# A two-layer hybrid decoder: one ordered set of weight tiles, another queue for blocks split ahead, and other part sizes in the middle of the FFN

## The chip, the cores and the metric

The kernel runs on one core of one Trainium2 chip. The metric is the device time of one execution in microseconds (us). Before the change it is 1271.52 us, the median of three runs (1269.11 to 1273.94).

## The reference, cut to what matters

Two layers, each a mixer sub-layer (attention, a Conformer convolution and a short gated convolution side by side) and a ConvGLU feed-forward network (FFN). 528 tokens (16 meta tokens and 512), width 1024, FFN width 2816, all in float32. The change lies in the FFN:

```python
D_MODEL, SEQ, N_META, DEPTH, D_FF, FFN_KERNEL = 1024, 512, 16, 2, 2816, 3

def ffn_sublayer(h, pre_g, post_g, w_up, conv_w, w_down):
    u = rms_norm(h, pre_g)
    z = jnp.einsum("bld,df->blf", u, w_up)            # (528, 5632)
    z = causal_depthwise_conv(z, conv_w)              # 3 taps
    g, up = jnp.split(z, 2, axis=-1)
    y = jnp.einsum("blf,fd->bld", jax.nn.silu(g) * up, w_down)
    return h + rms_norm(y, post_g)
...
    for l in range(DEPTH):
        h = mixer_sublayer(h, ...)
        h = ffn_sublayer(h, ...)
    return h[:, N_META:]
```

## The kernel before, in words

**Precision by halves.** Every float32 operand of a large product is split in two float32r tiles, a high part (a cast on ScalarE, ACT) and a low part (raw minus high, on VectorE, DVE). A product is three matmuls: high × high, low × high, high × low (`mm3`, L692). Weights arrive as blocks of 128 partitions × up to 1056 columns ("raw"), by DMA from one long array `wflat`, and are split on the way. Token columns lie in two halves of about 264.

**The order of the work** is made by a planner, `Flow` (L325 onwards): each operation of ACT, DVE, GpSimd and the DMA queues is given a planned cost, what it comes after, a priority and the ring slot that it takes, and is written out in the order in which the planner would run it. TensorE's work comes from generators ("threads"). The program order on each engine and queue is thus fixed in advance; on the chip, semaphores make each instruction wait for what it reads, and engines and queues run in order. `Ring` hands out buffers in turn, `Pick` (L202) the one that the plan has free first.

**The middle of the FFN** (`middle`, L2359) goes through the 22 pairs of gate and up blocks, in the order of `ORDERS`, in four parts of `PARTS` pairs:

- `u` is one plain up block: 48 matmuls, eight k × three products × two halves. Two of them make a pair (96 matmuls). The first two pairs are made before the middle starts (as `first`); the third (`h`) is made half by half as the normalised input u appears.
- `a` and `b` make a pair by a Strassen-Winograd scheme with seven products in place of eight: 7 × 12 = 84 matmuls (`eighth`, L2306). It needs weights X (one raw block), the sums Y and Z of quarter blocks (four DVE additions, L2199, into tile `z`), and W (half a raw block), each split in high and low, and four sums T of the input, made once a layer (`plan_t`, L2326, tiles `h` and `t_lo`). Between its products there are copies on ACT (L2454, L2460, L2469) and additions in PSUM on DVE (L2459, L2470, L2474).
- `D` is one of the eight blocks of the down projection for the part before: as many k as that part has pairs, added to `yp` by DVE (L2442).
- After each pair comes `gating` (L2249): two times (one tap on ACT, L2261, two on DVE, L2264) into one of four `c` tiles, SiLU (L2275), product (L2282, L2284), and the split into one of eight `g` tiles (yhi L2294, ylo L2298). A part's `g` tiles are given back with its eighth `D`.

The last part's down projection is made in `finish` (L1756), whose `products` follow the middle; post-norm, residual and the next layer's pre-norm are in it.

**Weights in the middle** are brought by `bring` (L2112; raw loads at L2120 on SyncE's queue, SPq, in three buffers `raw`) and split by `halves` (L2125; high L2132, low L2142) in five pairs of tiles (`general`), with a small ring for W (`wring`, the `acc` tiles) and one tile `z` for all four sums. `LOOK` is how many items ahead this is planned.

**Blocks split ahead.** In layer 1's middle, `split_ahead` (L2155) also splits the 22 blocks of layer 2's input projection, in 44 pieces: load `araw` (L2165), cast `ahi` (L2169), subtraction in place (L2173), and two stores to DRAM, `split_w` (L2175, L2177), all three DMAs on SPq. Two `araw` buffers and one `ahi` buffer turn over. Layer 2's mixer then fetches ready halves through GpSimd's queue (L636), which also carries other weights outside the middle (`plan_block`, L623). Two pieces are planned with each `D`.

**Between mixer and FFN**, `scaled_half` (L2040) makes u when the norm's factor rz is there: for each half 8 multiplications h × gain × rz on DVE (L2053), casts (L2056), subtractions (L2058). The residual h goes to DRAM (`h_mid`) and comes back for `finish`.

## Time and profile before

| | us |
|---|---|
| median of three runs | 1271.52 |
| the profiled execution, its own time | 1268.06 |
| its span, first to last instruction | 1266.3 |
| TensorE (PE) busy | 1230.4 |
| VectorE (DVE) busy | 1008.4 |
| ScalarE (ACT) busy | 709.3 |
| GpSimd (POOL) busy | 113.2 |

The mean granted clock of TensorE was 0.997 of full speed. Busy time of TensorE counts overlapping matmuls once, so a stretch that is all busy is told apart from a slow one by the number of matmuls in it. Layer 1's FFN starts at about 266 us and its Strassen pairs run from 322.67 to 578.28; layer 2's FFN starts at about 900 us. Rows of the profile name the line of the kernel, the engine, the operation and "written<-read" tiles; a queue's name ends in q (SPq, POOLq), and its rows are the issuing of DMAs.

### The profile page before, as it was taken

What the parts mean: (1) busy time and instruction counts of PE and PEld (TensorE: products, weight loads), DVE (VectorE), ACT (ScalarE), POOL (GpSimd) and SP (SyncE); (2) the same over time, 40 slices, a digit from 0 to 9 for tenths busy, and PEclk for the clock granted to TensorE, in tenths of its full rate; (3) what the DMA queues carried; (4) which work ended last, traced back from release to release, by engine and by line L of the source; (5) the groups of instructions that cost most, each with busy time, mean ns of one, the idle gap of its engine ahead of it and who ended that gap; (6) DMA issues with size and microseconds to landing.
All of it is one profiled execution on the core that took longest, in us unless ns stands there. A gap on an engine that the chain in (4) does not pass through costs nothing.

```text
span 1266.3 us, 24330 instructions
## 1 busy us (share of the span) xinstructions
PE 1230.4 (97%) x9552; PEld 1175.1 (93%) x9552; DVE 1008.4 (80%) x1785; ACT 709.3 (56%) x1389; POOL 113.2 (9%) x270
## 2 busy tenths in 40 slices
PE   9999999999999999989999999999999999999997
PEld 8988899989999999979999998999898998999897
DVE  7999986899978888876479985767998768887755
ACT  7446577666555555453563355776655444444543
POOL 1312210100000000000213133101000000000000
PEclk9999999999999999989999999999999999999999
DMA  7132123522476776665461652245222332323511
GB/s 253 51 86 77 52 76 119 184 85 88 154 250 231 227 234 219 220 236 191 163 254 34 195 154 78 88 145 184 69 80 84 125 101 75 106 90 99 189 58 67
DMA packets 75346, 173.22 MB, mean 137 GB/s; under 512 B 7984, under 2 KB 26672, under 8 KB 75232
## 3 DMA queue, kind: packets, MB, share of 16 engines
q1 hardware_dynamic: 61008, 119.01, 28.9%
q0 software_dynamic: 14080, 52.53, 12.8%
q8 instruction: 75, 1.23, 0.4%
q14 instruction: 39, 0.32, 0.1%
q10 hardware_dynamic: 144, 0.13, 0.1%
HBM read 135.49 MB, written 31.79 MB: 132 GB/s over the span
## 4 chain that ended last, share of the span: by engine, by line
PE 69%; DVE 18%; DMA 5%; ACT 4%; issue 3%; SPq 0%; DVEq 0%; ACTq 0%
PE psum L698 43%; PE psum L2310 14%; DVE c L2264 4%; PE psum L1325 3%; PE psum L1571 2%; DVE wlo L2142 2%; PE psum L1518 2%; DMA split_w<-ahi 2%; DVE z L2199 2%; DVE cacc L1044 2%; DMA raw<-in_w_dram 1%; DMA split_w<-araw 1%; PE psum L861 1%; PE psum L1473 1%; ACT whi L2132 1%
## 5 line engine op out<-in xcount | busy, mean ns | idle before, releaser
L698 PE MATMUL psum<-uhi,whi 128*128 128x264 f32 (+1 forms) x1120 | 288.4, 290 | 0.0
L698 PE MATMUL psum<-ulo,whi 128*128 128x264 f32 (+1 forms) x1120 | 281.5, 284 | 3.5 <-DVE ulo L2058 2.9
L698 PE MATMUL psum<-uhi,wlo 128*128 128x264 f32 (+1 forms) x1120 | 281.2, 284 | 0.0
L698 PE MATMUL psum<-yhi,whi 128*128 128x264 f32 (+3 forms) x928 | 260.3, 303 | 5.1 <-DVE c L2264 4.4
L698 PE MATMUL psum<-ylo,whi 128*128 128x264 f32 (+3 forms) x928 | 257.0, 300 | 1.5 <-DVE ylo L2298 1.1
L698 PE MATMUL psum<-yhi,wlo 128*128 128x264 f32 (+3 forms) x928 | 256.9, 299 | 0.6 <-DVE wlo L652 0.6
L698 PEld LDWEIGHTS psum<-ulo,whi 128*128 128x128 f32 x1120 | 196.0, 188 | 5.5 <-DVE ulo L2058 4.0
L698 PEld LDWEIGHTS psum<-uhi,whi 128*128 128x128 f32 x1120 | 196.3, 188 | 3.1 <-ACT uhi L2056 0.4
L698 PEld LDWEIGHTS psum<-uhi,wlo 128*128 128x128 f32 x1120 | 196.1, 188 | 0.0
L698 PEld LDWEIGHTS psum<-yhi,whi 128*128 128x128 f32 x928 | 166.5, 189 | 11.4 <-ACT rs L2460 4.8
L698 PEld LDWEIGHTS psum<-ylo,whi 128*128 128x128 f32 x928 | 166.5, 189 | 8.2 <-DVE ylo L2298 2.5
L698 PEld LDWEIGHTS psum<-yhi,wlo 128*128 128x128 f32 x928 | 166.5, 189 | 6.7 <-DVE wlo L652 1.2
L2264 DVE SCALAR_TENSOR_TENSOR c<-psum,pv,c 128x512 f32<-128x512 f32 (+2 forms) x160 | 117.8, 753 | 46.9 <-ACT c L2261 46.2
L636 POOL DMA_DIRECT2D raw<-in_w_dram x60 | 32.1, 536 | 911.9 <-DMA h<-h_mid 672.2
L2142 DVE TENSOR_TENSOR wlo<-raw,whi 128x1024 fp32r<-128x1024 f32 (+2 forms) x102 | 105.5, 1041 | 6.0 <-ACT whi L2132 5.8
L2132 ACT CAST whi<-raw 128x1024 fp32r<-128x1024 f32 (+2 forms) x102 | 92.0, 905 | 25.3 <-PE psum L698 17.2
L1044 DVE SCALAR_TENSOR_TENSOR cacc<-apad,pv,cacc 128x528 f32<-128x528 f32 x120 | 90.3, 766 | 1.2
L2261 ACT ACTIVATE c<-psum,pv 128x528 f32<-128x528 f32 (+1 forms) x80 | 55.0, 693 | 64.2 <-PE psum L2310 34.1
L652 DVE TENSOR_TENSOR wlo<-raw,whi 128x1024 fp32r<-128x1024 f32 (+3 forms) x66 | 74.6, 1142 | 17.8 <-ACT whi L646 17.5
L2310 PE MATMUL psum<-h,whi 128*128 128x264 f32 (+1 forms) x288 | 82.7, 287 | 5.8 <-ACT whi L2132 5.6
L2310 PE MATMUL psum<-h,wlo 128*128 128x264 f32 (+1 forms) x288 | 83.2, 289 | 5.2 <-DVE wlo L2142 5.1
L2310 PE MATMUL psum<-uhi,whi 128*128 128x264 f32 (+1 forms) x288 | 81.9, 284 | 0.9 <-DVE psum L2470 0.9
(263 smaller groups left out, 2589.1 us busy)
## 6 DMA issues: line engine op xcount, KB each, us to landing
raw<-in_w_dram SPq DMA_DIRECT2D x78, 512.0 KB, 3.6
raw<-in_w_dram POOLq DMA_DIRECT2D x44, 512.0 KB, 4.2
araw<-in_w_dram SPq DMA_DIRECT2D x40, 256.0 KB, 3.6
split_w<-ahi SPq DMA_DIRECT2D x40, 256.0 KB, 3.4
split_w<-araw SPq DMA_DIRECT2D x40, 256.0 KB, 4.3
raw<-in_w_dram SPq DMA_DIRECT2D x32, 320.0 KB, 2.9
whi<-split_w POOLq DMA_DIRECT2D x20, 512.0 KB, 4.7
wlo<-split_w POOLq DMA_DIRECT2D x20, 512.0 KB, 6.4
```

Source lines behind the costliest of these rows:

```text
L636: nc.gpsimd.dma_start(to, src)
L652: nc.vector.tensor_sub(box["lo"][:, a:z], box["raw"][:, a:z], box["hi"][:, a:z].bitcast(F32))
L698: nc.tensor.matmul(d, lhsT=w[a][:, k, cols], rhs=rhs(b, k, hf), start=start and i == 0 and p == 0, stop=stop and i == n - 1 and p == 2)
L1044: nc.vector.scalar_tensor_tensor(conv[j], in0=src, in1=conv[j], scalar=col("a_dw_w", CK * j + i), op0=ALU.mult, op1=ALU.add)
L1325: nc.tensor.matmul(ps[:n, :nw], lhsT=(uhi, ulo)[ui][:, k, P * b:P * b + n], rhs=w[wi][:, k % 4, :], start=k == 0 and p == 0, stop=k == KD ...
L1518: nc.tensor.matmul(s, lhsT=k[:, ka:ka + kn], rhs=q[:, s0:s1], start=i == 0, stop=i == 1)
L1571: nc.tensor.matmul(d[DH * e:DH * (e + 1)], lhsT=lhsT(hd), rhs=rhs(hd), start=start, stop=stop)
L2132: nc.scalar.copy(box["hi"], src())
L2142: b.tok = dve(dve_us(n), lambda: nc.vector.tensor_sub(box["lo"], src(), box["hi"].bitcast(F32)), c, prio=at(due_us + 1.0))
L2261: nc.scalar.activation(box["c"], src, AF.Copy, scale=wtap(2, t))
L2264: nc.vector.scalar_tensor_tensor(d, in0=src, scalar=wtap(i, t), in1=d, op0=ALU.mult, op1=ALU.add)
L2310: nc.tensor.matmul(dst, lhsT=w[a][:, k0 + k], rhs=rhs(b, k), start=start and k + p == 0, stop=stop and k == 3 and p == 2, skip_group_check ...
```

## The change

Part sizes go from 6, 5, 5, 6 to 5, 5, 5, 7. The number of Strassen pairs goes from 12 to 13 in layer 1 and from 12 to 15 in layer 2. A new letter `w` in the order says where two pieces are split ahead, in place of two with each `D`. The pieces' three DMAs go from SPq to GpSimd's queue. The weight tiles of the middle (raw, high, low and the half-size W) come from one set of 14 (15 in layer 2), and are taken in one order that is written down ahead from the planned begin of each item (`plan_order`): a take waits, in the plan, until the one before it in that order has been made. A load is planned `LOAD` before its item, sums `SUM` and high parts `HIGH` before it; a DMA's planned latency grows by `SLACK`. `LOOK` goes from 7 to 9. The one tile for the four sums becomes two (Z and Y apart). `scaled_half` multiplies by rz alone, two blocks at a time, on values already multiplied by the gain on ACT (`gained`, in `finish`). One weight block fewer is prepared before the middle. The last part's reload of h is planned after the last item of the middle instead of after the last Strassen pair.

```diff
-PARTS = (6, 5, 5, 6)
-ORDERS = [("uuuuuu", "aDbDaDbDaDbDuuaDbD", "aDbDaDbDaDbDuuaDbD", "aDbDaDbDaDbDaDbDuuuu"),
-          ("uuuuuu", "aDbDaDbDaDbDuuaDbD", "aDbDaDbDaDbDuuaDbD", "aDbDaDbDaDbDaDbDuuuu")]
-LOOK = 7
+PARTS = (5, 5, 5, 7)
+ORDERS = [("uuuu", "aDwbDwaDwbDwwaDwbDwwuwuwaDwbDwww", "aDwbDwaDwbDwaDwbDwuwuwaDwbDww", "aDbDaDbDaDbDaDbDaubuuu"),
+          ("uuuu", "aDbDaDbDaDbaDbaDbD", "aDbDaDbDaDbaDbaDbD", "aDbDaDbDaDbaDbaDbDuuuu")]
+LOOK = 9
+SLACK, LOAD, SUM, HIGH = 1.5, 16.0, 9.0, 7.0
...
     after_first = [next(i for i, c in enumerate(chunks) if ...) + FIRST["w_out"]
-                   + 3
+                   + 2
...
             def scaled_half(hf, r_at):
-                    fs = [dve(stt_us(n), lambda y=y, k=k, i=i: nc.vector.scalar_tensor_tensor(
-                        y[:, i, :], in0=h[:, k + i, a:z], scalar=g_u[:, k + i:k + i + 1], in1=rz[:, a:z],
-                        op0=ALU.mult, op1=ALU.mult), r_at, prio=1) for i in range(2)]
+                    fs = [dve(dve_us(2 * n), lambda y=y: nc.vector.tensor_mul(
+                        y, y, rz[:, a:z].unsqueeze(1).to_broadcast([P, 2, n])), r_at, *hg_at[hf, k], prio=1)]
...
             else:                                  # in finish, ends(hf)
+                for k in range(0, KD, 2):
+                    begun[hf, k] = gained(h, yp, a, z, k, gpre, out_at[hf, k], 0.9)
                 yield from norms.factor(("h", hf), n[hf], out=rz[:, a:z])
...
+            def place(buf, dt):
+                if buf < 9:
+                    return T(wp, [P, CHUNK], dt, f"{('raw', 'whi', 'wlo')[buf // 3]}{buf % 3}", 1)
+                if buf < 13:
+                    return T(wx[0], [P, WCHUNK], dt, f"{('whi', 'wlo')[(buf - 9) // 2]}{3 + (buf - 9) % 2}", 1)
+                if buf < 14:
+                    return T(fp, [P, 4 * H], dt, "acc", 1)
+                return T(t_pool[0], [P, WCHUNK], dt, f"more{buf}", 1)
+            def plan_order():
+                for j, (x, f, e) in enumerate(plan_list):
+                    w = begins[j]
+                    if x == "a":
+                        events.extend([(w - LOAD, j, "r0"), (w - LOAD, j, "r1"), (w - SUM, j, "xh"), (w - SUM, j, "xl"),
+                                       (w - HIGH, j, "zh"), (w - HIGH, j, "zl")])
+                    elif x == "b":
+                        events.extend([(w - HIGH, j, "yh"), (w - HIGH, j, "yl"), (w - HIGH + 2.0, j, "wt")])
+                    elif x == "d" or x == "u" and (f, e) not in early_up:
+                        events.extend([(w - LOAD, j, "r0"), (w - HIGH, j, "xh"), (w - HIGH, j, "xl")])
+                events.sort(key=lambda v: v[0])
+                for a, b in zip(events, events[1:]):
+                    turn[b[1:]] = a[1:]
+            def takes(j, key, slot):
+                before = turn[j, key]
+                wait = When(lambda: [] if before is None or before in taken else None)
+                return [wait], [(tiles[0], slot)]
+            def plain_block(j, i, when):
+                b = Block()
+                raw, s1, got, n = load(j, "r0", i, when - LOAD)
+                hi, s2, c = high(j, "xh", raw, n, when - HIGH, got)
+                until(b, s2, low(b, j, "xl", raw, hi, n, when - HIGH + 1.0, c))
+                s1.close(b.tok)
+                return b
...
             def split_ahead(due_us):
-                got = flow.op("sp", dma_us(z - a), load, prio=at(due_us), lat=dma_lat(z - a), takes=[(araws, slot)])
+                def queued(us, to, src, *after, **kw):
+                    def issue():
+                        flow.free["pool"] = max(flow.free.get("pool", 0.0), flow.now) + GP_DMA
+                        nc.gpsimd.dma_start(to(), src())
+                    return flow.op("wdma", dma_us(z - a), issue, after, prio=at(us), lat=dma_lat(z - a) + SLACK, **kw)
+                got = queued(due_us, raw, lambda: wflat[...][:, a:z], takes=[(araws, slot)])
...
-                hslot.close(flow.op("sp", ..., lambda: nc.sync.dma_start(home[i][0][:, a:z], box["hi"].bitcast(F32)), [d], ...))
-                slot.close(flow.op("sp", ..., lambda: nc.sync.dma_start(home[i][1][:, a:z], box["raw"]), [d], ...))
+                hslot.close(d, queued(due_us + 6.0, lambda: home[i][0][:, a:z], lambda: box["hi"].bitcast(F32), c))
+                slot.close(queued(due_us + 6.0, lambda: home[i][1][:, a:z], lambda: box["raw"], d))
...
                 elif x == "d":
-                    blocks[j] = plain_block(chunk_at["ffn_w_down", e, starts[f]], when)
-                    if l == 0:
-                        split_ahead(when)
-                        split_ahead(when + 2.0)
+                    blocks[j] = plain_block(j, chunk_at["ffn_w_down", e, starts[f]], when)
+                elif x == "w":
+                    split_ahead(when)
+                    split_ahead(when + 2.0)
...
             def middle():
-                        if j == last_b:
-                            wider[0].close()
-                            wx[1] = wider[0].enter_context(...)
-                            h_again.extend(load_h(fp, h_mid, 1.0))
-                            freed.append(p4)
+                        freed[:] = [p4]
                     yield
+                yield [*araws.slots, *ahis.slots]
+                wider[0].close()
+                wx[1] = wider[0].enter_context(...)
+                h_again.extend(load_h(fp, h_mid, 1.0))
```

More of the change, by code (lines that the diff above doesn't have):

```diff
@@ L809, in square @@
             if k == 0:
[L810 removed]
+                a = act(us, lambda: squares(lambda: self.acc_tile[:, slot.buf][:, :, :n]), *after,
                         prio=prio, takes=[(self.acc, slot)])
@@ L2147, in plain_block, with bring @@
-            def plain_block(i, due_us):
-                box, slot, got = bring(i, due_us - 12.0)
-                b = halves(lambda: box["raw"], chunks[i][3] * chunk_cols(chunks[i]), due_us - 6.0, got)
-                slot.close(b.tok)
+                def bring():
+                    box["t"] = took(j, key, slot, F32)[:, :sz]
+                    nc.sync.dma_start(box["t"], wflat[offs[i]:offs[i] + P * sz].rearrange("(p s) -> p s", p=P))
+                wait, take = takes(j, key, slot)
+                got = flow.op("sp", dma_us(sz), bring, wait, prio=at(due_us), lat=dma_lat(sz) + SLACK, takes=take)
@@ new lines, in load, with blocked, high, copy @@
+                return box, slot, got, sz
+            def blocked(t):
+                return t.rearrange("p (k n) -> p k n", n=P)
+            def high(j, key, src, n, due_us, *after):
+                box, slot = {}, Slot()
+                def copy():
+                    box["t"] = took(j, key, slot)[:, :n]
+                    nc.scalar.copy(box["t"], src["t"])
+                wait, take = takes(j, key, slot)
+                return box, slot, act(act_us(n), copy, *after, *wait, prio=at(due_us), takes=take)
@@ new lines, in low, with rest, until @@
+            def low(b, j, key, src, hi, n, due_us, *after):
+                slot = Slot()
+                wait, take = takes(j, key, slot)
+                def rest():
+                    lo = took(j, key, slot)[:, :n]
+                    nc.vector.tensor_sub(lo, src["t"], hi["t"].bitcast(F32))
+                    b.w = blocked(hi["t"]), blocked(lo)
+                b.tok = dve(dve_us(n), rest, *after, *wait, prio=at(due_us), takes=take)
+                return slot
+            def until(b, *slots):
+                for s in slots:
+                    s.close(b.slot)
@@ L2161, in split_ahead @@
                 box, slot, hslot = {}, Slot(), Slot()
-                def load():
-                    box["raw"] = T(t_pool[0], [P, CHUNK // 2], F32, "araw", 2)[:, :z - a]
-                    nc.sync.dma_start(box["raw"], wflat[offs[i]:offs[i] + P * sz].rearrange("(p s) -> p s", p=P)[:, a:z])
                 def high():
@@ L2192, in plan_item @@
                 elif x == "a":
-                    (b1, s1, got1), (b2, s2, got2) = (bring(chunk_at["ffn_w_up", f + NF * e, 0], when - 14.0) for e in range(2))
-                    box, zslot = {}, Slot()
-                    def summed(o, left, right, new=False):
-                        if new:
-                            box["s"] = T(fp, [P, 4, 2 + L], F32, "z", 1).rearrange("p a b -> p (a b)")
-                        nc.vector.tensor_add(box["s"][:, Q * o:Q * (o + 1)], left(), right())
-                    half = {name: (lambda b=b, o=o: b["raw"][:, Q * o:Q * (o + 1)])
-                            for name, b, o in (("11", b1, 0), ("12", b1, 1), ("21", b2, 0), ("22", b2, 1))}
@@ L2203, in plan_item @@
-                    sums = [lambda i=i: box["s"][:, Q * i:Q * (i + 1)] for i in range(4)]
-                    X = halves(lambda: b1["raw"], WCHUNK, when - 8.0, got1)
-                    sa = dve(dve_us(Q), lambda: summed(0, half["21"], half["22"], True), got2, prio=at(when - 8.0),
-                             takes=[(zring[0], zslot)])
-                    sc = dve(dve_us(Q), lambda: summed(1, half["21"], half["11"]), got1, sa, prio=at(when - 8.0))
-                    sb = dve(dve_us(Q), lambda: summed(2, sums[1], half["22"]), sc, prio=at(when - 7.9))
@@ L2209, in plan_item @@
-                    sd = dve(dve_us(Q), lambda: summed(3, sums[2], half["12"]), sb, prio=at(when - 7.9))
-                    Z = halves(lambda: box["s"][:, 2 * Q:4 * Q], WCHUNK, when - 6.0, sb, sd)
-                    s1.close(X.tok, sc, sd)
-                    quarters[f] = {"X": X, "Z": Z, "sums": (box, zslot, sa, sc, Z), "raw": (b2, s2)}
-                elif x == "b":
-                    q = quarters[f]
-                    box, zslot, sa, sc, Z = q["sums"]
-                    b2, s2 = q["raw"]
-                    q["Y"] = halves(lambda: box["s"][:, :2 * Q], WCHUNK, when - 6.0, sa, sc)
-                    zslot.close(q["Y"].tok, Z.tok)
-                    def small():
-                        return [T(fp, [P, 2, H], F32R, "acc", 2).rearrange("p a b -> p (a b)") for _ in range(2)]
-                    q["W"] = halves(lambda: b2["raw"][:, Q:], Q, when - 5.0, sa, ring=wring[0], tiles=small)
-                    s2.close(sa, sc, q["W"].tok)
+                    (r1, s1, got1, n), (r2, s2, got2, _) = (
+                        load(j, f"r{e}", chunk_at["ffn_w_up", f + NF * e, 0], when - LOAD) for e in range(2))
@@ L2503, in tile_hybrid_trunk @@
                        lambda k: y_at[k, 0] + y_at[k, 1], yp,
-                       gains("mix_post_g"), gains("ffn_pre_g"), SPLIT["w_out"], first, rz, scaled_half, early, middle())
+                       gains("mix_post_g"), gains("ffn_pre_g"), SPLIT["w_out"], first, rz, scaled_half, early, middle(), hg_at)
                 flow.yields = 2
-                flow.run(lambda: len(freed) and not flow.threads)
+                flow.run(lambda: len(h_again) and not flow.threads)
                 was = {s.buf: s for s in mids[0].slots}
```

161 lines of the change are left out of this document (97 added, 64 removed).

## The prediction

> **What bounds the kernel now.** I read the page's engine shares and chain first, then the busy time of each engine by stretch, then who waited for whom on TensorE and on SyncE's queue (SPq, which only issues DMAs), then the order of time at the places found.
>
> ```profile
> PE 1230.4 (97%) x9552; PEld 1175.1 (93%) x9552; DVE 1008.4 (80%) x1785; ACT 709.3 (56%) x1389; POOL 113.2 (9%) x270
> PE 69%; DVE 18%; DMA 5%; ACT 4%; issue 3%; SPq 0%; DVEq 0%; ACTq 0%
> 266.00:332.00 66.00, 63.51 (x505) 61.97 (x504) 64.50 (x98) 39.08 (x57) 0.00 (x0) 1.00 0.27 85
> 322.00:460.00 138.00, 133.34 (x1078) 131.66 (x1078) 113.49 (x164) 79.18 (x126) 0.00 (x0) 1.00 0.68 223
> 460.00:505.00 45.00, 45.00 (x371) 45.00 (x370) 37.68 (x55) 24.61 (x40) 0.00 (x0) 1.00 0.69 233
> 505.00:580.00 75.00, 66.73 (x517) 65.38 (x516) 58.59 (x87) 36.52 (x58) 0.00 (x0) 0.95 0.68 228
> 899.00:965.00 66.00, 63.26 (x495) 61.05 (x496) 63.99 (x99) 37.86 (x56) 0.00 (x0) 1.00 0.22 68
> 965.00:1043.00 78.00, 78.00 (x535) 72.52 (x535) 55.50 (x76) 38.99 (x59) 0.00 (x0) 1.00 0.36 113
> ```
>
> Columns: stretch, length, busy time (instructions) of PE, PEld, DVE, ACT, POOL, granted clock, DMA share, GB/s. TensorE is the bound: 371 matmuls in 45.00 us is 0.1213 us each with no gap. At that pace the 517 of 505–580 need 62.7 us, so 12.3 us are lost there, part of it as a lower clock (0.95); the 1078 of 322–460 need 130.8, so 7.2 are lost. Both lie in layer 1's FFN middle. Layer 2's (965–1043) has nearly no gaps. The two openings of the FFN (266–332, 899–965) differ: DVE is busy 64.50 and 63.99 of 66 us, so there DVE and TensorE are bounds side by side.
>
> Why 505–580 loses time:
>
> ```profile
> PE psum L2310 <- ACT whi L2132: 5.6, 2, 4.2
> ACT ahi L2169 <- DMA araw<-in_w_dram: 5.8, 2, 3.8
> ACT ahi L2169 <- DMA split_w<-ahi: 3.4, 2, 2.9
> SPq L2165 <- DMA split_w<-araw: 104.7, 40, 5.1
> SPq L2120 <- DVE z L2199: 13.6, 6, 11.0
> ```
>
> (Total us, times, longest.) TensorE waits for ScalarE's weight casts (whi). ScalarE takes its work in order and stands before `ahi`, the cast of a block split ahead for layer 2. That block's load and stores go out on SPq, which stood 104.7 us in all until a buffer's store had landed, before its next split-ahead load. The FFN's own weight loads (L2120) queue behind it.
>
> **The change, part by part.**
>
> *More Strassen pairs.* A plain up pair is 96 matmuls, a Strassen pair 84. The number goes from 12 to 13 in layer 1 and to 15 in layer 2: four pairs, 48 matmuls fewer.
>
> ```profile
> 578.28 35.07 PE psum L698 x288
> L2142 DVE TENSOR_TENSOR wlo<-z,whi 128x1024 fp32r<-128x1024 f32 x48 | 58.6, 1220 | 11.4 <-ACT whi L2132 11.3
> L2199 DVE TENSOR_TENSOR z<-z,raw 128x512 f32<-128x512 f32 x48 | 32.9, 686 | 0.6
> L2459 DVE TENSOR_TENSOR psum<-rs,psum 128x258 f32<-128x258 f32 x5 | 2.1, 429 | 0.1
> ```
>
> 35.07/288 = 0.1218 us each: **−5.8 us**, all on the path. The price lies on DVE: one more low part of 1.22, a small one and four sums of 0.69, three PSUM adds of about 0.43: some 6 us more per pair. In layer 2 a part like 965–1043 would go from 55.5 of 78 us to 61.5 of 76.5, or 80%. That is below the 84% (37.68 of 45.00) at which layer 1 ran without a gap in 460–505, so I cost it at nothing; without that cover it is 6 us × 4 pairs.
>
> *Blocks split ahead on GpSimd's queue.* 132 DMAs leave SPq, so the FFN's loads no longer wait behind a store, and GpSimd, with no work there (POOL 0.00 in the rows above), waits instead; behind it stand only other blocks and, after the middle, the last part's weight loads. The two `araw` buffers and the one `ahi` buffer stay, so ScalarE can still stand before `ahi`. The planner gives each transfer 1.5 us more (SLACK) and so puts the cast later. Bounds for 505–580: all 12.3 us come back, or a third (4), when ScalarE's 9.2 us of waits for `ahi` stay. The nearest row is 322–460, where the same work and the same queue cost 7.2 us, of which 2.2 and 0.8 have other causes (below): 4.2 in 138 us, or 2.3 in 75. I take **−10**; of the 4.2 themselves, which SPq causes only in part, **−1** (0 to −3).
>
> *Parts of 5 instead of 6 pairs first.*
>
> ```profile
> 1031.30 7.22 PE psum L2310 x60
> 1038.52 4.17 PE psum L698 x18
> 1039.25 1.31 ACT L2294 CAST yhi<-c 128x512 fp32r<-128x512 f32 x2
> 1044.50 1.27 ACT L2261 ACTIVATE c<-psum,pv 128x512 f32<-128x512 f32 x2
> PE psum L698 <- DVE c L2264: 4.4, 2, 2.2
> ```
>
> Part 1's last Strassen pair leaves TensorE at 1038.52, but its gating starts at 1044.50, and the next down block, which reads it, waits 2.2 us; the 4.4 are this place in both layers. The gating needs two of four `c` buffers; two earlier pairs hold them until they get a `g` tile, and there are eight `g` tiles, six held by part 0 up to its last down block (1038.52, then `yhi` at 1039.25). With five held, three are free for part 1, pair 4 holds two `c` and pair 5 has the other two. **−4.4**; between 0 (another holder is late next) and −5.2 with the two `ylo` waits behind it.
>
> *The opening of the FFN.* Part 0 loses a plain pair, which moves to the last part: 96 × 0.1218 = 11.7 us of TensorE work leave a stretch where DVE is full. What leaves DVE with it:
>
> ```profile
> L2142 DVE TENSOR_TENSOR wlo<-raw,whi 128x1024 fp32r<-128x1024 f32 (+1 forms) x9 | 10.4, 1159 | 0.0
> L2264 DVE SCALAR_TENSOR_TENSOR c<-psum,pv,c 128x527 f32<-128x527 f32 (+1 forms) x16 | 11.9, 760 | 0.0
> L2284 DVE TENSOR_TENSOR c<-c,c 128x528 f32<-128x528 f32 x6 | 4.2, 704 | 0.0
> L2298 DVE TENSOR_TENSOR ylo<-c,yhi 128x528 fp32r<-128x528 f32 x6 | 4.2, 703 | 0.0
> L2053 DVE SCALAR_TENSOR_TENSOR yp<-h,pg,rz 128x264 f32<-128x264 f32 x16 | 6.7, 488 | 0.0
> L2058 DVE TENSOR_TENSOR ulo<-yp,uhi 128x528 fp32r<-128x528 f32 x8 | 5.3, 705 | 0.6 <-ACT uhi L2056 0.6
> PE psum L2310 <- DVE wlo L2142: 0.8, 1, 0.8
> L1782 ACT ACTIVATE yp<-psum,pg 128x264 f32<-128x264 f32 (+1 forms) x32 | 13.8, 484 | 0.6 <-PE psum L698 0.6
> ```
>
> Busy time by count: 2 × 1.16 + 4 × 0.74 + 0.70 + 0.70 = 6.7 us. `scaled_half` replaces 16 multiplies (6.7) by 8 of the size of L2058 (5.3): 1.4. In layer 1 one split-ahead subtraction (0.7) goes to a later place. So DVE is done 8.8 us sooner in layer 1 and 8.1 in layer 2, TensorE 11.7, and the first Strassen pair waits already (0.8). TensorE stands 2.9 + 3.6 us more: **+6.5**. Bounds: 0, if DVE's order puts the first pair's weights ahead of all gating, and +10, if four taps (3.0) come before them. The gains that leave the multiply go to ScalarE, 16 of 0.484 a layer, at a priority ahead of the second half's squares; ScalarE is busy 39 of 66 us there. **+1**, 0 to +4.
>
> *Costed at nothing.* The weight tiles: 13 or so in rings become 14 (15) in one set; a Strassen pair with two down blocks takes 9 + 6 = 15 of them, about the old fill. The later reload of h (after the last item instead of the last Strassen pair): the next 210 matmuls, 25.6 us, run without it. The last part's seventh pair: 48 matmuls change places.
>
> Sum: −5.8 − 10 − 1 − 4.4 + 6.5 + 1 = **−13.7 us**. The profiled execution took 1268.06 us, which would become 1254.4; the median of the runs is 1271.52, 3.5 above it, and becomes **1257.8**.
>
> **The rivals.** (1) *The opening costs nothing*: DVE's order favours the pair. −20.2, 1251.3. For it: sums and low parts have due times of their own; against: DVE has no gap there.
>
> (2) *The end of layer 1's middle stays as it is.* The same bytes go through the same DMA engines, `araw` still has two buffers, and ScalarE still stands before `ahi` in order: term −10 becomes 0. −3.7, 1267.8, no change. For it: 9.2 us of waits for `ahi` in that stretch; against: SPq's 104.7 us. [...]
>
> (3) *The written tile order makes each pair wait.* One late load now holds up every take behind it, hi and low parts included. Place: the first matmuls of each of 28 Strassen pairs.
>
> ```profile
> PE psum L2310 <- DVE wlo L2142: 5.1, 7, 1.4
> ```
>
> At 5.1/7 = 0.73 us a pair this is 20.4 us: 1278.2, slower. It undoes the gain from 0.49 us a pair. Against: 15 takes on 14 tiles leave almost a whole stage of lead.
>
> (4) *GpSimd's queue is too slow for the blocks.*
>
> ```profile
> raw<-in_w_dram SPq DMA_DIRECT2D x78, 512.0 KB, 3.6
> raw<-in_w_dram POOLq DMA_DIRECT2D x44, 512.0 KB, 4.2
> split_w<-araw SPq DMA_DIRECT2D x40, 256.0 KB, 4.3
> wlo<-split_w POOLq DMA_DIRECT2D x20, 512.0 KB, 6.4
> L2173 DVE TENSOR_TENSOR araw<-araw,ahi 128x512 f32<-128x512 f32 x40 | 27.4, 686 | 16.8 <-ACT ahi L2169 16.8
> L2169 ACT CAST ahi<-araw 128x512 fp32r<-128x512 f32 x40 | 24.8, 620 | 26.1 <-DMA split_w<-ahi 19.4 <-DMA araw<-in_w_dram 6.7
> ```
>
> A buffer's turn is load + cast + subtract + store. At 4.2 and 4.3 it is 9.8 us, 4.9 a block with two buffers, 216 us for 44 blocks; at 6.4 for the store 6.0 and 262 us. Some 275 us are there: from about 311 (the first Strassen pair, 11.7 us sooner than now) to about 585 (the middle's last up block, now at 578.28 + 222 × 0.1218 = 605, less the 20 that leave it). At 7 us both ways it would be 337, 62 beyond; 25.6 of that is hidden, 36 show: 1294. It decides from 6.25 us a block. [...]
>
> **How the numbers follow.** About 0.5% (6.4 us) is what a measurement can tell from no change, so faster is below 1265.2. Chances: forecast 0.50 (own range 1252 to 1264), rival 1 0.18, rival 2 0.18, rival 3 0.09, rival 4 0.05. The best bounds of all terms give −26.3 (1245), the worst +4.2 (1276). 1248 to 1271 leaves out rivals 3 and 4 and a rim of the others. Faster 0.69 (forecast, rival 1), same 0.20 (rival 2, weak forms of 3), slower 0.11.
>
> **What would show it.** Right: 505–580's counterpart near 0.1213 us a matmul with the clock at 1.00; no SPq wait for `split_w`; no TensorE wait on `c` L2264's successor at the first part boundary; 48 matmuls fewer; a new TensorE wait of some 3 us for a low part or sum at each layer's first Strassen pair. Wrong: waits for low parts spread over all pairs (rival 3), ScalarE still standing before `ahi` (2), or GpSimd's stores running on past the middle (4).

## The result and the profile after

The changed kernel takes 1279.28 us (median of 8 runs, 1274.60 to 1287.50), the kernel before 1270.82 beside it (8 runs, 1269.09 to 1273.94): a ratio of 1.0069 with a 95% interval of 1.0043 to 1.0094. It is slower by 0.7%, where 1257.8 and faster were forecast. The profiled execution took 1279.28 us with a span of 1277.6, against 1268.06 and 1266.3; the mean granted clock went from 0.997 to 0.993.

The page after, engine shares and chain:

```profile
PE 1230.2 (96%) x9528; PEld 1175.7 (92%) x9528; DVE 1028.0 (80%) x1805; ACT 732.3 (57%) x1441; POOL 181.9 (14%) x401
PE 58%; DVE 16%; DMA 15%; issue 6%; ACT 3%; POOL 2%; SPq 0%; DVEq 0%; ACTq 0%; POOLq 0%
```

Fewer matmuls, as forecast, but TensorE's share of the chain fell from 69% to 58% and that of DMAs rose from 5% to 15%: the chain now runs through `split_w` stores. The stretches of the kernel before, and then those of the changed kernel, cut at like events (the end of the first Strassen pair's first waits, the end of the Strassen pairs):

```profile
250.00:330.00 80.00, 77.11 (x613) 75.42 (x613) 78.21 (x126) 48.79 (x79) 0.00 (x0) 1.00 0.28 89
330.00:578.00 248.00, 235.83 (x1888) 233.01 (x1887) 199.96 (x291) 131.81 (x209) 0.00 (x0) 0.99 0.69 228
578.00:610.00 32.00, 32.00 (x265) 32.00 (x264) 17.75 (x24) 12.79 (x18) 1.62 (x3) 1.00 0.41 131
```

```profile
250.00:325.00 75.00, 66.10 (x507) 63.97 (x506) 71.39 (x111) 49.42 (x88) 0.54 (x1) 0.98 0.24 81
325.00:585.00 260.00, 248.53 (x2008) 246.31 (x2007) 212.52 (x309) 141.01 (x224) 66.99 (x125) 0.99 0.67 217
585.00:620.00 35.00, 32.49 (x256) 32.31 (x255) 22.63 (x29) 18.18 (x27) 7.97 (x15) 0.96 0.59 190
```

The columns are those of the stretches in the prediction. Stretch length less matmuls × 0.1213 is what TensorE lost. Layer 1's opening: 80.0 − 613 × 0.1213 = 5.6 before, 75.0 − 507 × 0.1213 = 13.5 after. The Strassen pairs: 19.0 before, 16.4 after. The start of `finish`: 3.9 after (585–620) and nothing before (578–610). In layer 2 matmuls of two widths are mixed, so there the table takes, from the start times of all matmuls, the time between two starts beyond that of the width at full pace (0.122 us for 264 columns, the median in both traces, and 0.225 for 512, the 5th percentile in both; the median there is 0.232 before and 0.233 after, with which layer 2's Strassen pairs lose some 2 us less in both kernels); it is the same to about 1 us in layer 1. Where exactly a stretch is cut moves its figure by up to 1 us as well. Two kernels of the experiments below stand beside it.

| TensorE time lost, us | before | after | high stores on SyncE (e1) | and u as before (e14) |
|---|---|---|---|---|
| layer 1, opening | 5.3 | 13.4 | 12.6 | 12.6 |
| layer 1, Strassen pairs | 18.0 | 15.4 | 5.7 | 1.9 |
| layer 1, start of finish | 0.5 | 5.1 | 5.0 | 4.8 |
| layer 2, opening | 6.6 | 15.8 | 15.6 | 13.1 |
| layer 2, Strassen pairs | 7.4 | 3.2 | 3.5 | 3.6 |

After minus before: +8.1 − 2.6 + 4.6 + 9.2 − 4.2 = +15.1, with the matmuls' −5.8 and some +1.7 at the very end +11.0; the spans differ by 11.3. So three things happened: both openings lost 17 us more, layer 1's Strassen pairs gave back next to nothing, and a new wait appeared at `finish`.

Who waits for whom, after:

```profile
PE psum L2392 <- DVE raw L2195: 4.1, 3, 2.2
PE psum L699 <- DVE raw L2195: 3.3, 2, 3.1
PE psum L699 <- DVE whi L2195: 3.2, 1, 3.2
PE psum L699 <- ACT yhi L2376: 3.0, 1, 3.0
PE psum L699 <- DVE yp L1777: 2.7, 2, 2.5
PE psum L2392 <- DVE wlo L2195: 2.2, 1, 2.2
POOL araw L2231 <- DMA split_w<-araw: 114.2, 31, 7.1
ACT ahi L2225 <- DMA split_w<-ahi: 41.3, 20, 5.6
```

L699 is a plain product, L2392 a Strassen one, L2195 the low part (it now lands in tiles named raw, whi, wlo or acc alike). The 3.2 and 3.1 are the first plain block after `h` in each opening, the 2.2 of `raw` and of `wlo` the low part of Z in the first Strassen pair. SPq waits for no `split_w` any more, as forecast; GpSimd does, for 114.2 us (SPq before: 104.7), and ScalarE stands 41.3 us before `ahi` where it stood 24.8.

How that reaches TensorE, at 494 us (the order of time on POOL, ACT and PE):

```profile
486.06 0.54 POOL L2231 DMA_DIRECT2D split_w<-araw  x1
489.50 0.62 ACT L2225 CAST ahi<-araw 128x512 fp32r<-128x512 f32 x1
493.68 0.55 POOL L2231 DMA_DIRECT2D araw<-in_w_dram  x1 [7.07 <-issue]
494.22 0.54 POOL L2231 DMA_DIRECT2D split_w<-ahi  x1
498.15 0.62 ACT L2225 CAST ahi<-araw 128x512 fp32r<-128x512 f32 x1 [5.12 <-DMA split_w<-ahi]
498.68 0.63 ACT L2376 CAST yhi<-c 128x528 fp32r<-128x528 f32 x1
499.36 0.51 PE L699 MATMUL psum<-yhi,whi 128*128 128x264 f32 x2 [2.96 <-ACT yhi L2376]
```

`ahi` was cast by 490.1, but its store is issued only at 494.22, behind the load ahead of it in GpSimd's queue, which waits until an `araw` buffer's low part (the store issued at 486.06) has landed. The store of `ahi` lands at about 498; with one `ahi` buffer the next cast waits until then, `yhi` waits behind that cast on ScalarE, and TensorE waits for `yhi`. The profile names no releaser for this one load's 7.07 us: the semaphore events of the trace have the low part landed at 490.8, so the last 2.9 us before the load have another cause, which is open. Of the other loads 31, 114.2 us in all, are put down to that landing.

### The profile page after: what moved, and what is told of

Same layout as the page of the kernel before. It is cut to its first block, busy times and chain, and to the rows that moved or that the text cites. A ratio compares the mean times of both kernels' runs of the same rounds, so it can differ in the third digit from the quotient of the medians.

```text
span 1277.6 us, 24350 instructions
## 1 busy us (share of the span) xinstructions
PE 1230.2 (96%) x9528; PEld 1175.7 (92%) x9528; DVE 1028.0 (80%) x1805; ACT 732.3 (57%) x1441; POOL 181.9 (14%) x401
## 4 chain that ended last, share of the span: by engine, by line
PE 58%; DVE 16%; DMA 15%; issue 6%; ACT 3%; POOL 2%; SPq 0%; DVEq 0%; ACTq 0%; POOLq 0%
PE psum L699 33%; PE psum L2392 13%; DMA split_w<-araw 7%; DMA split_w<-ahi 4%; PE psum L1327 3%; PE psum L1573 2%; PE psum L1520 2%; DVE c L2346 2%; DMA raw<-in_w_dram 2%; DVE cacc L1046 2%; PE psum L1475 1%; DMA araw<-in_w_dram 1%; POOL araw L2231 1%; DVE acc L818 1%; POOL split_w L2231 1%
## 5 line engine op out<-in xcount | busy, mean ns | idle before, releaser
L699 PE MATMUL psum<-uhi,whi 128*128 128x264 f32 (+1 forms) x864 | 235.4, 292 | 3.6 <-DVE whi L2195 3.2
L699 PE MATMUL psum<-yhi,whi 128*128 128x264 f32 (+3 forms) x806 | 229.9, 302 | 6.3 <-ACT yhi L2376 3.0
L699 PE MATMUL psum<-uhi,wlo 128*128 128x264 f32 (+1 forms) x864 | 228.1, 284 | 0.4 <-DMA wlo<-split_w 0.4
L699 PE MATMUL psum<-yhi,wlo 128*128 128x264 f32 (+3 forms) x792 | 222.5, 299 | 3.5 <-DVE wlo L653 1.8
L699 PE MATMUL psum<-ulo,whi 128*128 128x264 f32 (+1 forms) x816 | 219.9, 284 | 1.3 <-DVE ulo L2064 1.1
L699 PE MATMUL psum<-ylo,whi 128*128 128x264 f32 (+3 forms) x634 | 180.7, 293 | 0.4 <-DVE ylo L2380 0.3
L699 PEld LDWEIGHTS psum<-uhi,whi 128*128 128x128 f32 x864 | 155.6, 188 | 6.6 <-DVE whi L2195 3.4
L699 PEld LDWEIGHTS psum<-yhi,whi 128*128 128x128 f32 x806 | 148.1, 190 | 12.1 <-ACT yhi L2376 3.2
L699 PEld LDWEIGHTS psum<-uhi,wlo 128*128 128x128 f32 x864 | 155.7, 188 | 0.6 <-DMA wlo<-split_w 0.6
L699 PEld LDWEIGHTS psum<-yhi,wlo 128*128 128x128 f32 x792 | 145.4, 190 | 8.2 <-DVE wlo L653 2.5
L699 PEld LDWEIGHTS psum<-ulo,whi 128*128 128x128 f32 x816 | 148.9, 188 | 2.6 <-DVE ulo L2064 1.5
L699 PEld LDWEIGHTS psum<-ylo,whi 128*128 128x128 f32 x634 | 118.6, 190 | 3.0 <-DVE ylo L2380 0.5
L2392 PE MATMUL psum<-h,whi 128*128 128x264 f32 (+1 forms) x376 | 92.6, 287 | 1.6 <-DVE c L2346 0.7
L653 DVE TENSOR_TENSOR wlo<-raw,whi 128x1024 fp32r<-128x1024 f32 (+3 forms) x64 | 74.0, 1165 | 17.3 <-ACT whi L647 16.7
L2392 PE MATMUL psum<-h,wlo 128*128 128x264 f32 (+1 forms) x300 | 79.8, 288 | 4.0 <-DVE wlo L2195 2.2
L647 ACT CAST whi<-raw 128x1024 fp32r<-128x1024 f32 (+3 forms) x64 | 63.7, 1002 | 15.9 <-DMA raw<-in_w_dram 14.2
L2392 PEld LDWEIGHTS psum<-h,whi 128*128 128x128 f32 x376 | 67.2, 192 | 2.4 <-ACT rs L2547 0.9
L2392 PE MATMUL psum<-uhi,whi 128*128 128x264 f32 (+1 forms) x224 | 59.8, 284 | 2.4 <-DVE psum L2557 2.4
```

The source lines that it names most:

```text
L647: nc.scalar.copy(box["hi"][:, a:z], box["raw"][:, a:z])
L653: nc.vector.tensor_sub(box["lo"][:, a:z], box["raw"][:, a:z], box["hi"][:, a:z].bitcast(F32))
L699: nc.tensor.matmul(d, lhsT=w[a][:, k, cols], rhs=rhs(b, k, hf), start=start and i == 0 and p == 0, stop=stop and i == n - 1 and p == 2)
L2392: nc.tensor.matmul(dst, lhsT=w[a][:, k0 + k], rhs=rhs(b, k), start=start and k + p == 0, stop=stop and k == 3 and p == 2, skip_group_check ...
```

## The experiments

Each ratio is to the kernel before, run on the same chip.

**e1, the high parts' stores on SyncE.** One of the three DMAs of a piece leaves GpSimd's queue:

```diff
-hslot.close(d, queued(due_us + 6.0, lambda: home[i][0][:, a:z], lambda: box["hi"].bitcast(F32), c))
+hslot.close(d, flow.op("sp", dma_us(z - a), lambda: nc.sync.dma_start(home[i][0][:, a:z], box["hi"].bitcast(F32)),
+                       [c], prio=at(due_us + 6.0), lat=dma_lat(z - a) + SLACK))
```

> The changed kernel, with one of the three DMAs of a block split ahead, the store of its high part (split_w<-ahi), issued on SyncE's queue; the load and the low part's store stay on GpSimd's. Theory A (GpSimd's queue stands before the next araw load until a low part has landed, the high part's store queues behind that load, so ahi comes free late and ScalarE, in order, stands before the next cast): ScalarE's waits for ahi on split_w fall from 41 us to under 15, layer 1's Strassen stretch loses some 8 us less, time about 1271 us. Rival (the written tile order makes the waits, and ScalarE's stand is only beside it): ScalarE's waits fall, TensorE's stay, time within 2 us of the changed kernel's 1279.

1267.44 us, ratio 0.9968 [0.9952, 0.9984]: 12 us less than the changed kernel. Layer 1's Strassen pairs lose 5.7 us instead of 15.4. The rows of ScalarE:

```profile
ACT ahi L2225 <- DMA araw<-in_w_dram: 21.4, 14, 3.2
ACT ahi L2225 <- DMA split_w<-ahi: 9.1, 6, 2.7
```

The wait for the store falls from 41.3 to 9.1, as theory A had it; the wait for the load grows from 8.4 to 21.4, so ScalarE still stands some 30 us before `ahi`. The pieces are the same (44 high stores, 256 or 264 KB each); only the queue that issues them differs: from 290 to 600 us queue q0 moved 33.92 MB in the changed kernel and 23.99 in e1, q1 27.40 and 38.74. The gain lies in not standing behind a DMA that waits. (SPq's 104.7 us before the change are of this kind too, waits for a landing and not issuing time.)

**e2, u made as before** (16 fused multiplies on DVE, no gains on ScalarE ahead of the second half's squares):

```diff
-begun[hf, k] = gained(h, yp, a, z, k, gpre, out_at[hf, k], 0.9)
+begun[hf, k] = []
...
-fs = [dve(dve_us(2 * n), lambda y=y: nc.vector.tensor_mul(y, y, rz[:, a:z]...), r_at, *hg_at[hf, k], prio=1)]
+fs = [dve(stt_us(n), lambda ...: nc.vector.scalar_tensor_tensor(... g_u ... rz ...), r_at, prio=1) for i in range(2)]
```

> The changed kernel with the making of u as before: 16 multiplies h x gain x rz on VectorE, no gains ahead on ScalarE. Theory B (the gains run ahead of the second half's squares on ScalarE, so that half's norm factor comes some 6 to 9 us late, and VectorE stands idle in a stretch in which it is the bound): the second half's rz comes back by 6 us or more in both layers, the idle time of 2.7 us before it goes, time about 1274. Rival (the opening is late only because a plain pair left it; VectorE's work decides): VectorE has 1.4 us more per layer, time 1279 to 1282.

1277.29 us, ratio 1.0056 [1.0031, 1.0081]: 2 us, not 5, and not clear of the noise, as the interval overlaps that of the changed kernel. The second half's statistics reach DVE 6.7 us earlier in layer 1 (269.02 instead of 275.71), but TensorE still waited 3.4 and 3.3 us for the same two low parts.

**e3, parts of before in the changed kernel**, and **e4, the new parts and orders alone in the kernel before** (with its rings):

```diff
-PARTS = (5, 5, 5, 7)
+PARTS = (6, 5, 5, 6)
-ORDERS = [("uuuu", "aDwbDwaDwbDwwaDwbDwwuwuwaDwbDwww", "aDwbDwaDwbDwaDwbDwuwuwaDwbDww", "aDbDaDbDaDbDaDbDaubuuu"), ...]
+ORDERS = [("uuuuuu", "aDwbDwaDwbDwaDwbDwuuaDwbDw", "aDwbDwaDwbDwaDwbDwuuaDwbDw", "aDwbDwaDwbDwaDwbDwaDbDuuuu"), ...]
```

This is e3 in layer 1; layer 2 gets the orders of before. It also spreads the blocks split ahead: the letters `w` stand 8, 8 and 6 in parts 1 to 3, where the changed kernel has 14 and 11 in parts 1 and 2. e4 goes the other way, without any `w`: there two pieces still come with each `D`.

> The changed kernel with parts of 6, 5, 5, 6 and 12 Strassen pairs per layer, the blocks split ahead two after each down block of parts 1, 2 and half of 3; all else as changed. Theory B2 (most of the loss of the opening, 17 us over what the moved pair should give, comes from the moved pair): the opening gives back about 11 us, 48 more matmuls cost 5.8, the boundary waits come back with 4.4: about 1278, with the first Strassen pair waiting under 1 us. Rival (the opening's loss comes from the gains and the order of weights, the parts pay as forecast): 1279 + 5.8 + 4.4 - 6.5 = 1283.

> The kernel before with parts of 5, 5, 5, 7 and 13 and 15 Strassen pairs alone (blocks split ahead with each down block, as before). By the forecast's terms -5.8 - 4.4 + 6.5 = -3.7: 1267 us. By theory B2 the opening costs 11 instead of 6.5: about 1272. In both the wait of 2.2 us at the first part boundary is gone and 48 matmuls fewer run; if that wait is still there, the reading with eight g tiles falls.

e3: 1271.48 us, ratio 1.0002 [0.9985, 1.0018]. e4: 1310.94 us, ratio 1.0316 [1.0290, 1.0342]. In e3 the waits on `c` at the part boundaries are back, the 3 us waits of the openings have stayed, and ScalarE stands before `ahi` as long as in the changed kernel; in e4 no wait on `c` is left, but the Strassen pairs wait for their weights:

```profile
PE psum L699 <- DVE c L2346: 7.0, 4, 2.2
PE psum L699 <- DVE whi L2195: 3.2, 1, 3.2
PE psum L699 <- DVE raw L2195: 3.1, 1, 3.1
ACT ahi L2225 <- DMA split_w<-ahi: 42.1, 17, 5.1
```

```profile
PE psum L2310 <- DVE wlo L2142: 26.0, 26, 2.4
PE psum L2310 <- ACT whi L2132: 16.4, 15, 4.5
```

Both missed what was expected of them, e3 by 7 us on the fast side and e4 by 39 us on the slow side. The four kernels together, lost time reckoned as in the table above:

| TensorE time lost, us | before | new parts alone (e4) | all but the parts (e3) | both (changed) |
|---|---|---|---|---|
| both openings | 12 | 26 | 18 | 29 |
| layer 1, Strassen pairs | 18 | 40 | 11 | 15 |

So the new parts and orders cost the openings 14 or 11 us, and the rest of the change 6 or 3. With the orders of before, GpSimd's queue and the new tiles do give layer 1's Strassen pairs 7 us back. The rings of before can't feed the denser order (40 us lost); which of the tiles, `LOOK`, the due times and the queue makes it possible was not tried apart.

**e5, one weight block more prepared early, as before the change:**

```diff
-after_first = [... + FIRST["w_out"] + 2
+after_first = [... + FIRST["w_out"] + 3
```

> The changed kernel with one edit: one more weight block is prepared before the middle begins (three chunks after the first, as before the change, in place of two). Theory C: the two waits of PE at L699 on the block prepared late in the opening (3.2 us on whi in layer 1 and 3.3 us on raw in layer 2) go, and with the second the half-clock stretch that follows it (about 1.7 us lost); the later waits of the first Strassen pair on its low part (1.5 + 2.4 and 0.7 + 2.3 us) stay or shrink. 1279 less 6 to 8: about 1272, ratio to the kernel before 1.001. Rival: VectorE is the bound of the whole opening, so that the wait only moves from the plain block to the first Strassen pair, which then waits 3 us longer in each layer: about 1279, ratio 1.007.

1284.32 us, ratio 1.0090 [1.0060, 1.0120]. The plain block's wait goes, and others come:

```profile
PE psum L699 <- ACT whi L647: 7.2, 2, 4.6
PE psum L863 <- DVE acc L818: 5.7, 3, 2.7
PE psum L2392 <- DVE whi L2195: 3.0, 1, 3.0
PE psum L2392 <- DVE more L2195: 2.9, 1, 2.9
PE psum L2392 <- DVE raw L2195: 1.9, 1, 1.9
```

Theory C falls, its rival stands: the wait moved to the statistics (L863, 3.5 us in the changed kernel) and to the first Strassen pair. The first row is not of the openings: it is a wait of 4.6 us at 619.4 and one of 2.7 at 1238.5, in `finish`. The mean granted clock fell to 0.982: by the start times of the matmuls, half clock cost 15 us in this execution and 7 in the changed kernel's, while the waits add up to the same within some 1 us. So the loss against the changed kernel lies in the clock.

**e6, the raw buffers of `finish` from the tiles that come free first:**

```diff
-raws.slots = deque(held(i, bufs[i]) for i in range(3))
+o = sorted(range(9), key=lambda i: (bufs[i].time is None, bufs[i].time or 0.0, i))
+raws.slots = deque(held(i, bufs[o[i]]) for i in range(3))
...
```

> The changed kernel with one edit: at the end of the middle the three raw buffers of the plain preparation are taken from those three of the nine tiles that come free first, in place of three fixed ones that the last pairs' weights still hold. Theory D: the load of the next raw chunks no longer waits 11.5 us for PE, and the wait of 2.7 us at 613 with the half-clock stretch behind it (1.7 us), and the 1.3 us wait of layer 2's finish, go: 4 to 5 us, about 1274.5, ratio 1.003. Rival: the finish waits for VectorE's other work (the additions of the last products) whatever the buffers are: 1279, ratio 1.007, with the wait at the finish still 2 us or more.

1281.92 us, ratio 1.0075 [1.0049, 1.0101]. The first load is issued 12 us earlier than in the changed kernel (603.74), but the cast that needs it comes right behind the last gating's `yhi` in both (in the changed kernel at 607.37, behind `yhi` at 606.56):

```profile
591.75 0.54 POOL L637 DMA_DIRECT2D whi<-in_w_dram  x1
605.31 0.63 ACT L2376 CAST yhi<-c 128x528 fp32r<-128x528 f32 x1 [2.38 <-DVE c L2366]
605.85 0.94 ACT L647 CAST raw<-whi 128x896 fp32r<-128x896 f32 x1
```

```profile
PE psum L699 <- DVE yp L1777: 4.6, 2, 2.5
```

TensorE's waits for the sums at `finish` (the last row, both layers) are longer than the 2.7 of the changed kernel. Theory D falls; that a shorter gating at the end would free it was not tried.

**e7, the edits of e1, e5 and e6 together**, and **e8, with Z's low part ahead of the taps as well:**

```diff
-until(Z, s6, low(Z, j, "zl", z, zh, WCHUNK, when - HIGH + 1.5, z_at))
+until(Z, s6, low(Z, j, "zl", z, zh, WCHUNK, when - HIGH + 0.5 - 2.0 * (j == ...), z_at))
```

The term cut short is 2.0 for the first Strassen pair and 0 for the others.

> The changed kernel with three edits at once: the high parts' stores on SyncE, one more block prepared early, and the raw buffers of the finish from the tiles that come free first. If the three causes stand apart, the gains add: 1267.4 less 6 to 8 less 4 to 5, about 1256, ratio 0.988, which is near the sum that was forecast (1257.8). If the opening or the finish is bound by VectorE all the same, it stays near 1265, ratio 0.996.

> The three edits, and the low part of the first Strassen pair's second operand is computed on VectorE ahead of the four gating multiplications that stood before it. Theory: PE's wait at the first Strassen pair on that low part (2.4 and 2.3 us, with the waits on the pair's weights 1.5 and 0.7 us before it) shrinks by about 2 us in each layer: 4 us less than the kernel with the three edits alone, about 1252, ratio 0.985. Rival: the gating multiplications are then late themselves, or the weights' low part takes the wait's place: no difference from the three edits, 1256.

1270.40 us, ratio 0.9983 [0.9965, 1.0001], and 1270.74, ratio 0.9979 [0.9962, 0.9996]: nothing on top of e1. In e7 the first Strassen pair waits 3.0 us in each layer for X's low part (`whi` and `more`, L2195), and then 1.5 and 1.9 us for Z's. In e8 the waits for Z's are gone, those for X's have stayed, and the time is the same. So far each edit of the order in the opening had removed one wait without shortening the time, which asks for a test of the amount of work on DVE (theory E).

**e9, e1 and the four sums of the input's quarters on GpSimd**, and **e12, that with the parts of before:**

```diff
-nc.vector.tensor_sub(quad(0), quad(0), quad(1))   # and three more, planned on DVE
+nc.gpsimd.tensor_sub(quad(0), quad(0), quad(1))   # and three more, planned on GpSimd
```

> The changed kernel with the high parts' stores on SyncE (1267.4 before), and the four sums of the quarters of the activations (L2429 to L2432, 1.24 us each on VectorE in the opening of each layer's FFN) computed on GpSimd. Theory E: VectorE sets the pace of the whole opening, which is why the early block moved the wait and did not remove it. Then 5.0 us less work on it per layer makes the waits before and at the first Strassen pair 5 us shorter per layer (3.4 + 2.4 and 3.2 + 2.4 us now; the first comes before the sums and may stay), so at least the two of 2.4 us and the half-clock stretch behind one of them go: about 1261, ratio 0.992. Rival: GpSimd is slow enough (over 3 us a sum) that the product of the first sums itself comes late, or slows VectorE beside it: 1267 or more, ratio 0.997 or above.

> The stores on SyncE, the parts and orders of before, and the four sums on GpSimd. With six plain pairs the first Strassen pair already comes later, and no wait was left there, so that the sums cost TensorE little: theory E in this order gives 0 to 3 us beside the kernel without the sums moved, about 1258, ratio 0.989. Rival: VectorE's relief is passed on to all that follows it in the opening: 1254, ratio 0.986; or GpSimd in the way, 1262.

1277.78 us, ratio 1.0044 [1.0024, 1.0063], and 1287.14, ratio 1.0118 [1.0092, 1.0144]. Layer 2's opening in e9, then layer 1's same DVE row in e1 and in e9 and the wait that it causes:

```profile
917.97 2.94 POOL L2430 TENSOR_TENSOR yp<-yp 128x1032 f32<-128x1032 f32 x1 [44.40 <-DVE ulo L2064]
920.99 2.74 POOL L2431 TENSOR_TENSOR yp<-yp 128x1032 f32<-128x1032 f32 x1
923.81 2.34 POOL L2432 TENSOR_TENSOR yp<-yp 128x1032 f32<-128x1032 f32 x1
926.23 2.35 POOL L2433 TENSOR_TENSOR yp<-yp 128x1032 f32<-128x1032 f32 x1
918.95 11.50 DVE L2347 SCALAR_TENSOR_TENSOR c<-z,pv,c 128x512 f32<-128x512 f32 x6
```

```profile
283.03 4.16 DVE L2347 SCALAR_TENSOR_TENSOR c<-z,pv,c 128x528 f32<-128x528 f32 x6
```

```profile
287.29 8.53 DVE L2347 SCALAR_TENSOR_TENSOR c<-z,pv,c 128x528 f32<-128x528 f32 x6
299.60 0.81 PE L699 MATMUL psum<-uhi,whi 128*128 128x264 f32 x2 [7.92 <-DVE whi L2195]
```

GpSimd needs 2.3 to 2.9 us for a sum that takes DVE 1.24, and while it runs DVE's taps on two SBUF operands take two to three times their time (8.53 and 11.50 us for six in e9, 4.16 in e1). TensorE's wait before the plain block grows from 3.2 to 7.9. The rivals of both expectations, GpSimd in the way, hold, and with more than their price in e12.

**e13, e1 with the four sums left out** (nothing takes their place, so this kernel computes something else):

```diff
-last = dve(us, fn, *(ready if last is None else [last]), prio=at(when + 2.0 * i))
+last = last or dve(0.1, lambda: nc.vector.tensor_sub(quad(0)[:, :1, :8], ...), *ready, prio=at(when))
```

> The changed kernel with the high parts' stores on SyncE (1267.4, ratio 0.997), and the four sums of the quarters left out (only a corner of 8 columns of one is computed, 0.1 us): the products of the first Strassen pairs multiply the unsummed quarters, with the same instructions on every other engine. Nothing runs on GpSimd in its place. Theory E, VectorE sets the pace of the whole opening: 5 us less work on it per layer; the wait of 3.4 us before the plain block stays, since it comes before the sums; the 2.4 us at the first Strassen pair go in both layers with the half-clock stretch after one of them, about 1261, ratio 0.992. Rival: the waits there come from the order alone (the taps ahead of the low part), so they stay: 1267, ratio 0.997.

1261.76 us, ratio 0.9892 [0.9869, 0.9916]; e1 had 0.9968. The plain block's wait has stayed, the waits for Z's low part are gone, and by 325 us TensorE is 31 matmuls (3.8 us) further than in e1 (the first row; e13 is the second):

```profile
250.00:325.00 75.00, 67.01 (x513) 64.87 (x512) 71.02 (x110) 49.26 (x88) 0.00 (x0) 0.98 0.25 81
```

```profile
250.00:325.00 75.00, 69.80 (x544) 68.30 (x543) 70.80 (x115) 51.72 (x91) 2.14 (x4) 0.98 0.28 94
```

Theory E stands: with less work on DVE both openings lose less (9 and 11 us by the reckoning of the table, 12.6 and 15.6 in e1), and slowing DVE (e9) lengthened them (18 and 18). DVE's work is not all that counts, though: making u as before, which gives DVE more work, takes 2.5 us off layer 2's opening (e14 in the table).

**e10, e1 with the parts of before; e11, that with u as before; e14, e1 with u as before (new parts); e15, e14 with Z's low part first.** The edits are those above.

> The changed kernel with the high parts' stores on SyncE and the parts and orders of before (6, 5, 5, 6 and 12 pairs). Alone the stores gave 12 us and the old parts 8. Theory F: the two stand apart (queue in the middle of layer 1, VectorE in the openings): 1279.3 less 12 less 8, about 1259.5, ratio 0.990, and the new parts are a loss even with the queue mended. Rival: the denser order of the new parts is what suffered from the queue, so that mending it makes up for both: 1267, ratio 0.997, equal to the new parts with the stores on SyncE.

> As the one before, and the u of the pre-norm made as before (16 fused multiplies on VectorE, no gains on ScalarE): only the weight tiles in a written order, the split-ahead DMAs and the one block fewer prepared early are left of the change. Theory: the gains alone were worth 2 us when undone: about 1257.5, ratio 0.989. Rival: with six plain pairs in the opening the two multiplies more per k pair make VectorE later still: 1262 or more.

> The new parts, the high parts' stores on SyncE, and u made as before (no gains on ScalarE). With the old parts this step gave 2 us (1268.9 to 1267.0), and with all stores on GpSimd's queue also 2. If it adds: 1265.4, ratio 0.995, as fast as the old parts with the same two edits, so that the 48 matmuls taken away are worth nothing net. Rival: without the queue's waits the denser order shows its 5.8 us after all: 1261, ratio 0.992.

> As the one before, with the low part of the first Strassen pair's Z ahead of the taps. If the order there matters, the waits of 2.4 us go and it comes to 1261 to 1263; if VectorE is the bound, another wait takes their place, as with the three edits together: 1265.4, ratio 0.995.

| | parts | u | us | ratio to before |
|---|---|---|---|---|
| e10 | before | changed | 1268.86 | 0.9980 [0.9966, 0.9995] |
| e11 | before | as before | 1266.99 | 0.9954 [0.9936, 0.9973] |
| e1 | new | changed | 1267.44 | 0.9968 [0.9952, 0.9984] |
| e14 | new | as before | 1262.48 | 0.9909 [0.9886, 0.9932] |
| e15 | new | as before | 1266.84 | 0.9932 [0.9909, 0.9955] |

Theory F falls: the parts and the queue do not stand apart. On GpSimd's queue the new parts and orders cost 7.8 us (e3 against the changed kernel); moving the high stores to SyncE gives 12 us with them (e1) and 2.6 without (e3 to e10). With the high stores on SyncE and u as before the new parts gain: 0.9954 − 0.9909 is 0.45%, 5.7 us (e11 and e14 are of different sets of runs, so this is less sure than a ratio to before; against e15, which differs from e14 in one low part's order, it would be 0.2%, within the intervals). With u as changed they gain nothing clear (e1 and e10). e14 is the best of the kernels that leave nothing out, faster than both, as the rival of its expectation had it. The stretch that the prediction started from is full in it:

```profile
460.00:580.00 120.00, 118.67 (x969) 117.83 (x968) 107.03 (x155) 68.25 (x108) 21.60 (x40) 1.00 0.72 240
```

120.00/969 = 0.1238 us a matmul at clock 1.00, against 0.1213 at full pace. e15 adds nothing to e14, like e8 to e7.

## Why the prediction was wrong, point by point

- **48 matmuls fewer, −5.8: right.** The Strassen matmuls go from 12 × 84 to 13 × 84 in layer 1 and 15 × 84 in layer 2. The page counts only 24 fewer (9552, 9528), because the last part's seventh pair in layer 2 is done as 48 matmuls of 256 columns, where 24 of 512 did it before. TensorE's work at full pace fell by 5.5 us by the same reckoning as the table.
- **Blocks on GpSimd's queue, −10 and −1: the first step that failed.** SPq stopped waiting for `split_w`, as forecast, but with the boundary's share of about 2.2 the Strassen pairs of layer 1 were to lose 13 us less and lost 2.6 less. The sentence that failed is that behind the waiting GpSimd there "stand only other blocks": the high part's store stands there too, on which the single `ahi` buffer and, through ScalarE's order, TensorE depend. Rival 2 named ScalarE before `ahi`, but held its wait fixed at 9.2 us in that stretch; over the run the wait for the store grew from 24.8 to 41.3. Once that store is elsewhere, 12.3 of the 13 are there (e1: 5.7 lost instead of 18.0; 1.9 in e14, but about 7 in e15, so some us are scatter). The store behind the load is not the whole of it: in e3 it stands there as well and ScalarE waits 42.1 us, yet the Strassen pairs lose 11 us, not 15, and moving the store gives 2.6 us instead of 12. It is dear only with the new orders, which the prediction priced as if they stood apart from the queue. Whether the larger number of Strassen pairs or the closer letters `w` do it stays open.
- **The opening, +6.5 and +1: the second step that failed.** The mechanism, DVE as the bound, was right (e13, e9); the size was +17.3 (8.1 and 9.2). By e3 and e4 the new parts alone cost 11 to 14 of it, over the upper bound of 10 for the first term, and the rest of the change 3 to 6, where +1 was forecast; how that divides between the gains, the tiles' order and the missing early block is not shown. DVE was to be done 8.8 us sooner in layer 1; it ended Z's low part at 320.1 instead of 325.2, 5.1 us sooner, with 2.7 us idle for the statistics of the second half that the gains had pushed back, and the four taps of the upper bound did come before Z's low part. TensorE has 96 matmuls (11.7 us) less before it, so 6.6 of layer 1's 8.1 follow from that. The granted clock fell as well: 1.2 us were lost behind a wait in layer 1's opening and 1.6 behind each of two in layer 2's, which no term held. The missing early block was not costed at all; putting it back (e5) did not shorten the time.
- **The first part boundary, −4.4: right.** The wait on `c` is gone in the changed kernel (0.7 us of such waits, at another place), it is there in e3 with the old parts (7.0) and not in e4 with the new ones, and layer 2's Strassen pairs lose 3.2 instead of 7.4.
- **Gains on ScalarE, +1 within 0 to +4:** 2 by e2 (not clear of the noise), 2 to 3 by e10 and e11 with the parts of before, 5.0 (medians) to 7.5 (ratios) by e1 and e14; above the bound in the last.
- **Costed at nothing:** the tiles were rightly so in the middle: no wait is spread over the pairs (rival 3 falls). At `finish` 4.6 us are lost that no term held. The parts don't cause it: e3, with those of before, loses about 4 us there too, and e4, with the new parts and the old rings, next to nothing. The last pairs' weights hold the raw buffers there, but freeing them (e6) did not give the time back, so which of the remaining edits it is, and what a remedy would be, stays open.
- **Rival 1** (a free opening) and **rival 4** (stores past the middle) fall: the last `split_w` store is issued at 591.7, and the weight loads behind it go out only at 603.74, after a wait for TensorE. That rival 3's 1278.2 lies near the measured time is chance: its mechanism is not there. Of the two signs named for rival 2, the half that came true was ScalarE before `ahi`.

## What to carry to other kernels

Before moving DMAs to another engine's queue, list for each one what stands ahead of it there and what that waits for; a store that frees a single buffer must not stand behind a load that waits for another buffer (ScalarE waited 41.3 us for the store here, and 9.1 with it on another queue). Where two engines are full side by side, a change that takes work from one is priced by what leaves the other in the same stretch, and reordering inside it mostly moves the wait. Two edits that are worth nothing or less apart can gain together (the new parts with and without the mended queue), so undo parts in pairs before dropping one.
